# Encoder trunk: the output stages take the two products for the second half of the tokens last, sum them over all blocks in PSUM, and keep their weight forms in DRAM

## The chip, the cores and the metric

One core of one Trainium2 chip. The metric is device time in microseconds for one execution of the whole kernel. The engines are named as in the profile: PE (TensorE), DVE (VectorE), ACT (ScalarE), POOL (GpSimd), SP (SyncE, which issues most DMAs). Three runs of the kernel before gave 2766.35, 2768.74 and 2769.79 us; the median is 2768.74.

## What is computed

Two layers of an encoder on x of shape (1, 1024 tokens, 1024 channels) in float32. The first layer mixes tokens by grouped-query attention (16 heads of 64, 4 key/value heads), the second by a chunked gMLP of width 6144. Each is followed by a dense MLP of hidden width 4096 with a squared ReLU. Every sublayer is preceded by an RMS norm and modulated by vectors that are worked out from the conditioning vector c.

```
for i in range(2):
    mod = silu(c) @ ada_w[i] + ada_b[i]
    sh1, sc1, g1, sh2, sc2, g2 = split(mod, 6)
    h = modulate(rmsnorm(x, norm1_g[i]), sh1, sc1)
    y = gqa_attention(h, ...) if i == 0 else chunked_gmlp(h, ...)
    x = x + g1 * y
    h = modulate(rmsnorm(x, norm2_g[i]), sh2, sc2)
    x = x + g2 * (square(relu(h @ w_in[i])) @ w_out[i])
```

## The kernel before

Every large matmul is done as three products of rounded halves: each float32 operand is split into a rounded part hi (a cast on ACT) and a remainder lo (a subtraction on DVE or POOL), and hi·hi, hi·lo and lo·hi are summed. Around these stands a scheme with seven block products in place of eight (as Strassen and Winograd have it): forms of the operands are added up beforehand, seven products named 1 to 7 are taken, and their sums give the four quarters of the result.

The stages follow each other: QKV, attention, the output projection (`wo`), MLP0's first matmul, MLP0's `Out`, the gMLP's two input products (v, then u), the gMLP's `Out`, MLP1's first matmul, MLP1's `Out`.

**`Out` (L963 to L1110)** is used three times: for MLP0 and MLP1 with 4 blocks of the contraction, for the gMLP with 3. It works in units of 12 matmuls (4 tiles of the contraction times three products; 2.72 us each where TensorE isn't held up, by the starts of successive units in the trace). A unit is named by block b, product q and output pair p of 4. `ahead` issues what is due some units early: `load_w` and `load_w2` fetch the four quarters of a block's weights (11, 12, 21, 22); `prep`, three units ahead (LO), makes the form that the product needs on POOL (L1031 to L1036) and splits it (ACT L1041, DVE L1042); `load_f` and `split_f` fetch a form of the hidden activations from DRAM, eight units ahead, and split it five units ahead (ACT L287, DVE L288). Split activations live in the buffers named t, of which there are 58. `run` issues the matmuls (L1056 hi·hi, L1057 hi·lo, L1058 lo·hi) and `take` (L1082 to L1110) adds a product to the residual x through `add` (L1069, DVE) or to an accumulator in SBUF (L1084, DVE; for the first block an ACT copy). Products 1, 2, 6, 4, 7 serve the first half of the tokens (half 0), and 6 and 7 half 1 as well; 5 and 3 serve half 1 alone. For the blocks ahead of the last two the order is 1264753; the last two take 12647 each, and then 5 and 3 in turns of the two, summed in PSUM. So the last 16 units are the tail: half 0 is complete there, and its next norm begins. `norm_hook` (L1226) does that: at unit HK = 1 of the tail the sums of squares go through TensorE (`norm_ss`, L244, with squares summed on POOL at L235) and DVE (L246 and on), two units later the result is spread over the partitions (`norm_rb`, L255), and then the forms for the next stage are made a step at a time.

**`Slabs` (L159 to L199)** works out four groups of modulation vectors in the attention loop: 4 groups of 8 steps, each a DMA of 512 KB (SP), a multiplication (POOL L184) and an addition (POOL L185, none in a group's first step), and 8 one-column matmuls at a group's end (L194).

**The attention loop (L920 to L956)** runs over 64 units of one head and one pair of query blocks. The order of the work in a unit is written out in the string `ORDER`: near its end stand q (`q_stage`, POOL L811 and L812, in units 1, 5, 9, ...: the split queries that are transposed in the two units from the next one on), f (`f_stage`, POOL L887, a sum of two parts of the output), and m (`slabs.step`). `q_trans` (PE L820) stands early in a unit. Near the end the loop also issues the loads of x (L463) and the first weights of `wo` (L105, cast by ACT at L108).

SP issues DMAs in the order of the program, and waits in it for what a DMA needs. Modulation vectors that are not yet needed stand in `pending` and are made by `mods`, a DMA and two DVE operations of which L145 is the long one, in places written out for each stage (MO: in MLP0's `Out` one in every third unit from the 14th).

Of the kernel before, what the change touches and what calls it, by code (L numbers as in the profile page):

```python
# [11 lines left out]
F32 = mybir.dt.float32  # L12
# [6 lines left out]
P = 128  # L19
# [17 lines left out]
def encoder_kernel(ctx: ExitStack, tc: tile.TileContext, t: dict, out: bass.AP):  # L37
# [121 lines left out]
    class Slabs:  # L159
# [11 lines left out]
        def step(self, bank):  # L171
            self.n += 1
            if self.ends and self.n >= self.ends[0][0]:
                self.end(self.ends.pop(0)[1], bank)
            if not self.work:
                return
            self.ahead(3)
            g, dt = self.work.pop(0)
            raw = self.raw.pop((g, dt))
            if dt == 0:  # L180
                self.acc[g] = wide("s")
                pin(G.tensor_scalar(self.acc[g], raw, condc[:, 0:1], None, ALU.mult))
            else:
                pin(G.tensor_scalar(raw, raw, condc[:, dt : dt + 1], None, ALU.mult))  # L184
                pin(G.tensor_tensor(self.acc[g], self.acc[g], raw, ALU.add))  # L185
            if dt == KT - 1:
                self.ends.append((self.n + 2, g))

        def end(self, g, bank):
            layer, j = g  # L190
# [611 lines left out]
    with ExitStack() as es:  # L802
# [117 lines left out]
        for i in range(nu + 2):  # L920
            u0 = units[i] if i < nu else None
            u1 = units[i - 1] if 0 < i <= nu else None
            u2 = units[i - 2] if i > 1 else None
            if u0:
                if i % 4 == 0:
                    qst, nxt = nxt, []
                u0.qst = qst
            for op in ORDER.split():
                f, w, j = op[0], int(op[1]), int(op[2])
                if f == "m":  # L930
                    if deferred:
                        deferred.pop(0)()
                    elif WO_AT <= i < WO_AT + 10:
                        if i == WO_AT:
                            load_sel()
                        elif i == WO_AT + 1:
                            wo_sums(0)
                        else:
                            wo_prep(0, i - WO_AT - 2)
                    elif i >= nu:  # L940
                        mods(1)
                    if i % 2 or i >= nu:
                        slabs.step(bank_x)
                elif f == "q":
                    if i % 4 == 1 and w == 0 and i + 3 < nu:
                        qh = q_stage(units[i + 3].qq, units[i + 3].g)
                    if i % 4 > 1 and w == 1 and i + 2 < nu:
                        q_trans(qh, i % 4 - 2, nxt)
                else:
                    u = (u0, u1, u2)[w]  # L950
                    if u and (i or f not in "se"):
                        stages[f](u, j)
            if i == nu - 1:
                x[0] = [load_x(0, k) for k in range(KT)]
            if i == nu:
                wo_mm(0, (0,), bank_x)  # L956
# [2 lines left out]

    es_a.close()  # L960
    p_y = ctx.enter_context(tc.tile_pool(name="p_y", bufs=4, space=PSUM))

    class Out:  # L963

# [4 lines left out]
        def __init__(self, wsrc, forms, nblk, gate):  # L969
            self.wsrc, self.forms, self.nblk, self.gate = wsrc, forms, nblk, gate  # L970
            self.n = 28 * nblk
            self.w, self.raw, self.f, self.sf, self.acc = {}, {}, {}, {}, {}
            self.last2 = last2 = (nblk - 2, nblk - 1)
# [16 lines left out]
            tiles = []  # L990
            for i in range(0, self.n - 16, 4):
                tiles += [(i + kt, self.units[i][:2] + (kt,)) for kt in range(4)]
            for i in (self.n - 16, self.n - 8):
                tiles += [(i + 4 * j + kt - FM, (b, self.units[i][1], kt)) for j, b in enumerate(last2) for kt in range(4)]
            for i, k in tiles:
                at(i - FS - FA, self.load_f, k)
            for i, k in tiles:
                at(i - FS, self.split_f, k)
# [28 lines left out]
        def prep(self, i):  # L1027
            b, q, p = self.units[i]
            a11, a12, a21, a22 = (self.w.get((b, c, p)) for c in ("11", "12", "21", "22"))
            if q == "6":  # L1030
                G.tensor_tensor(a21, a21, a22, ALU.add)  # L1031
                G.tensor_tensor(a11, a21, a11, ALU.subtract)
            elif q == "4":
                G.tensor_tensor(a12, a12, a11, ALU.subtract)
            elif q == "7":
                G.tensor_tensor(a22, a22, a11, ALU.subtract)  # L1036
            src = {"1": a11, "2": a12, "6": a11, "4": a22, "7": a22, "5": a21, "3": a12}[q]
# [6 lines left out]
        def run(self, hook=None, done=None):  # L1044
            for i in range(self.n):
                self.ahead(i)
                b, q, p = self.units[i]
                hi, lo = self.sf.pop(i)
                two = q in "53" and b in self.last2
                begin, end = not two or b == self.last2[0], not two or b == self.last2[1]  # L1050
                if begin:
                    ps = (bank_x, bank_y)[(i // 2 if two else i) % 2]("out")
                for kt in range(4):
                    th, tl = self.f[(b, q, kt)]
                    a = slice(kt * P, (kt + 1) * P)
                    T.matmul(ps, hi[:, a], th, start=begin and kt == 0, stop=False)  # L1056
                    T.matmul(ps, hi[:, a], tl, start=False, stop=False)  # L1057
                    T.matmul(ps, lo[:, a], th, start=False, stop=end and kt == 3)  # L1058
                j = i - self.n + 16
# [11 lines left out]
        def take(self, i, b, q, p, ps, done):  # L1071
            acc = self.acc

            def add(hf, j, v):
                self.add(hf, j, p, v)

            if b < self.nblk - 1:
                if q in "243":
                    add(*{"2": (0, 0), "4": (0, 1), "3": (1, 0)}[q], ps)
                elif b == 0:  # L1080
                    acc[(q, p)] = slot()
                    S.copy(acc[(q, p)], ps)  # L1082
                else:
                    V.tensor_tensor(acc[(q, p)], ps, acc[(q, p)], ALU.add)  # L1084
                return
            a1, a6, a5, a7 = (acc[(c, p)] for c in "1657")
            if q == "1":
                V.tensor_tensor(a1, ps, a1, ALU.add)
                add(0, 0, a1)
# [6 lines left out]
                G.tensor_tensor(a7, a7, a6, ALU.add)  # L1096
            elif q == "4":
                add(0, 1, ps)
            elif q == "7":
# [3 lines left out]
            elif q == "5":  # L1103
                V.tensor_tensor(a5, ps, a5, ALU.add)
                add(1, 0, a5)
                add(1, 1, a5)
                done(1, 2 * p + 1)
            else:
                add(1, 0, ps)
                done(1, 2 * p)  # L1110

    OUT_FORMS = "1234567"


    dram = ctx.enter_context(tc.tile_pool(name="dram", bufs=1, space=bass.MemoryType.DRAM))

    def spread(tiles, dst, spare, eng):

# [15 lines left out]
    def mlp(layer, f, sqB, done, hook):  # L1134
# [42 lines left out]
        def at_out(i):  # L1177
# [48 lines left out]
    def norm_hook(layer, which, bank):  # L1226
        dg = []

        def hook(m):
# [161 lines left out]
    def gmlp(f, sqB, done, hook):  # L1391
# [116 lines left out]
        XL = {2: (0, 1), 6: (1, 0), 10: (1, 1)}  # L1508

        def at_out(i):  # L1510
            if i == CUT:
                cut(4)
            if i in XL:
                load_xs(*XL[i])
            if i >= out_.n - 16:
                hook(i - out_.n + 16)

        out_.run(at_out, done)

# [19 lines left out]
FS = 5  # L1539
FA = 3  # L1540
LO = 3
FM = 4
TG = ((0, 0), (1, 0), (1, 1), (0, 1))
MO = (14, 3, 1)
CUT = 8
LW = 5
IG = 30
SW = 3
WA = 6
LW2 = 2  # L1550
HK = 1
HB = 2
HBV = 2
WO_AT = 53
MODS = 32
RO = 1
RQ = 3
RW = 2
NA = (7,)
# [74 lines left out]
```

## Time and profile before

The profiled execution took 2778.2 us (its span in the trace is 2776.4), 9.5 us more than the median of the other three. Its mean TensorE clock was 0.978 of full speed.

| stage | from, us | to, us |
|---|---|---|
| QKV | 0 | 190 |
| attention | 190 | 579 |
| wo | 579 | 693 |
| MLP0 first matmul | 693 | 1015 |
| MLP0 Out | 1015 | 1346.5 |
| gMLP v | 1346.5 | 1596 |
| gMLP u | 1596 | 1877 |
| gMLP Out | 1877 | 2138.8 |
| MLP1 first matmul | 2138.8 | 2460.3 |
| MLP1 Out | 2460.3 | 2776.4 |

A row of a timeline gives the start in us, the duration in us, the engine, the line of the kernel, the operation, its output and inputs with their tiles, the count of like instructions put together, and in brackets the idle time ahead of it and what ended that. A row of waits gives the total, the number of times and the longest. A row of a stretch gives its length, then busy time and count for PE, PEld (weight loads), DVE, ACT and POOL, then the granted clock, the DMA share and GB/s.

### The profile page before, as it was taken

The page shows a single profiled execution, that of the slowest core. Times are in us where ns is not written, and L with a number is a line of the kernel's source. Part 1 is how long each engine was busy: PE and PEld are TensorE (multiplying, and loading weights), DVE is VectorE, ACT ScalarE, POOL GpSimd, SP SyncE. Part 2 cuts the span into 40 slices and gives each one's busy share as a digit, 9 for nine tenths or more (in the row PEclk, how much of TensorE's full clock was granted, in tenths as well). Part 3 has the DMA queues.
Part 4 walks back from the last instruction along what each step waited for, and adds up shares of the span by engine and source line. Part 5 has one row for each costly group of instructions (what it writes and reads, how often), then busy time and mean ns, then how long its engine had stood idle before and what let it go on. Part 6 is the DMA issues. An engine that isn't in the chain of part 4 may idle for free. (4 is left out here: it accounts for less than half of the span.)

```text
span 2776.4 us, 37109 instructions
## 1 busy us (share of the span) xinstructions
PE 2653.8 (96%) x12804; PEld 2195.6 (79%) x12804; DVE 2300.5 (83%) x3231; ACT 1450.6 (52%) x2608; POOL 1054.3 (38%) x716
## 2 busy tenths in 40 slices
PE   7889999999899999998899999999998999999998
PEld 5668999978688888786778888887876688888887
DVE  7889888878887788999997767786899887788896
ACT  4448999954544455434443354444435554554432
POOL 2446666654300023253543255555452400033351
PEclk9999999989999999999999999999998999999999
DMA  7131111235164465734243345555522264465541
GB/s 262 67 137 39 47 47 47 94 113 183 59 211 152 163 235 190 250 112 139 76 137 129 107 164 178 179 196 210 193 84 80 88 208 163 144 247 167 166 136 70
DMA packets 181967, 393.42 MB, mean 142 GB/s; under 512 B 21073, under 2 KB 33361, under 8 KB 181778
## 3 DMA queue, kind: packets, MB, share of 16 engines
q1 hardware_dynamic: 154898, 353.29, 37.6%
q10 hardware_dynamic: 26880, 37.76, 3.7%
q8 instruction: 101, 1.65, 0.2%
q14 instruction: 88, 0.72, 0.1%
HBM read 289.26 MB, written 101.71 MB: 141 GB/s over the span
## 5 line engine op out<-in xcount | busy, mean ns | idle before, releaser
L1057 PE MATMUL out<-t,s 128*128 128x512 f32 x1232 | 487.7, 396 | 14.4 <-DVE t L288 14.2
L1058 PE MATMUL out<-t,s 128*128 128x512 f32 x1232 | 485.6, 394 | 8.3 <-DVE s L1042 8.1
L1056 PE MATMUL out<-t,s 128*128 128x512 f32 x1232 | 484.7, 394 | 3.3 <-ACT t L287 3.3
L415 PE MATMUL w<-t,s 128*128 128x512 f32 x1168 | 460.0, 395 | 0.5 <-ACT t L287 0.5
L416 PE MATMUL w<-t,s 128*128 128x512 f32 x1168 | 455.4, 390 | 1.5 <-DVE t L288 1.3
L417 PE MATMUL w<-t,s 128*128 128x512 f32 x1168 | 454.8, 389 | 0.9 <-DVE s L401 0.9
L288 DVE TENSOR_TENSOR t<-t,t 128x512 fp32r<-128x512 f32 x408 | 383.7, 951 | 42.6 <-ACT t L287 28.9
L287 ACT CAST t<-t 128x512 fp32r<-128x512 f32 x408 | 244.6, 617 | 191.3 <-DVE t L288 80.5
L1031 POOL TENSOR_TENSOR w<-w,t 128x512 f32<-128x512 f32 x32 | 52.8, 1656 | 656.6 <-DMA t<-in_wm_dram 494.3
L1057 PEld LDWEIGHTS out<-t,s 128*128 128x128 f32 x1232 | 234.1, 190 | 70.8 <-DVE t L288 21.6
L1058 PEld LDWEIGHTS out<-t,s 128*128 128x128 f32 x1232 | 234.4, 190 | 61.7 <-DVE s L1042 12.9
L401 DVE TENSOR_TENSOR s<-w,s 128x512 fp32r<-128x512 f32 x292 | 229.5, 794 | 63.2 <-ACT s L400 62.9
L400 ACT CAST s<-w 128x512 fp32r<-128x512 f32 x292 | 172.8, 617 | 200.4 <-PE w L417 123.3
L1056 PEld LDWEIGHTS out<-t,s 128*128 128x128 f32 x1232 | 234.4, 190 | 53.9 <-ACT t L287 5.1
L416 PEld LDWEIGHTS w<-t,s 128*128 128x128 f32 x1168 | 219.4, 188 | 51.4 <-DVE t L288 6.6
L415 PEld LDWEIGHTS w<-t,s 128*128 128x128 f32 x1168 | 219.2, 188 | 49.4 <-issue 3.1
L417 PEld LDWEIGHTS w<-t,s 128*128 128x128 f32 x1168 | 219.2, 188 | 46.3 <-DVE s L401 1.3
L860 DVE TENSOR_TENSOR t<-t,t 128x512 fp32r<-128x512 f32 x256 | 164.0, 681 | 23.5 <-ACT t L854 23.4
L837 DVE TENSOR_REDUCE mx<-s 128x1 f32<-128x1024 f32 x128 | 156.4, 1222 | 27.9 <-PE s L834 26.9
L1042 DVE TENSOR_TENSOR s<-t,s 128x512 fp32r<-128x512 f32 x176 | 163.8, 931 | 15.1 <-ACT s L1041 14.6
L870 PE MATMUL o<-t,t 128*128 128x256 f32 x1024 | 164.9, 294 | 0.0
L851 PE MATMUL t<-ident,c 128*128 128x128 f32 x1024 | 152.4, 278 | 12.7 <-DVE t L860 7.5
(248 smaller groups left out, 5524.9 us busy)
## 6 DMA issues: line engine op xcount, KB each, us to landing
t<-hf SPq DMA_DIRECT2D x320, 256.0 KB, 4.4
hf<-c SPq DMA_DIRECT2D x156, 256.0 KB, 2.1
w<-in_wi_dram SPq DMA_DIRECT2D x64, 512.0 KB, 3.8
hf<-c ACTq DMA_DIRECT2D x96, 256.0 KB, 2.0
c<-in_ada_dram SPq DMA_DIRECT2D x36, 512.0 KB, 3.8
w<-in_adan_dram SPq DMA_DIRECT2D x32, 512.0 KB, 3.3
t<-in_wm_dram SPq DMA_DIRECT2D x64, 256.0 KB, 4.7
w<-in_ada_dram SPq DMA_DIRECT2D x28, 512.0 KB, 4.2
```

What stands on the lines that cost most here:

```text
L287: S.copy(hi, src)
L288: (eng or V).tensor_tensor(lo, src, f32(hi), ALU.subtract)
L400: S.copy(hi, src)
L401: V.tensor_tensor(lo, src, f32(hi), ALU.subtract)
L415: T.matmul(ps, hi[:, a], th, start=kt == 0, stop=False)
L416: T.matmul(ps, hi[:, a], tl, start=False, stop=False)
L417: T.matmul(ps, lo[:, a], th, start=False, stop=kt == 3)
L860: pin(V.tensor_tensor(lo, pt, f32(hi), ALU.subtract))
L870: pin(T.matmul(u.po, vt[st][:, u.g * P : (u.g + 1) * P], src[:, s * 256 : (s + 1) * 256], start=st == 0 and part == 0, stop=st == 7 and pa ...
L1056: T.matmul(ps, hi[:, a], th, start=begin and kt == 0, stop=False)
L1057: T.matmul(ps, hi[:, a], tl, start=False, stop=False)
L1058: T.matmul(ps, lo[:, a], th, start=False, stop=end and kt == 3)
```

## The change

1. **`Out`'s order.** All blocks take 12647 first; then come product 5 over all blocks, the last block first, and product 3 likewise. Each of their four output pairs is summed over the blocks in one PSUM bank that is held through the phase (four of bank_x for 5, four of bank_y for 3). The tail is now 8 units for each block: 32, 24 and 32.
2. **Kept weight forms.** Forms 5 and 3 are made together with 6 and 4, as before, but for all blocks except the last they are stored to DRAM at that time (`keep`) and loaded again 7 units ahead of use (`load_kept`, LK = 4): 24, 16 and 24 stores of 256 KB, and as many loads. Through the sum in PSUM 12 ACT copies and 40 DVE additions are no longer there.
3. **The norm hook.** It begins at unit 3 of the tail (HK) and makes a step of the next stage's forms every second unit to the end.
4. **Slabs.** `step` is called in every unit and works in those with `i * 5 % 8 < 5`, not in the odd ones; a group's end comes three calls later instead of two.
5. **Modulations.** Four of the 16 pending ones move from MLP0's `Out` to the gMLP's (MG).

```
-            if not self.work:
+            if not go or not self.work:
...
-                self.ends.append((self.n + 2, g))
+                self.ends.append((self.n + 3, g))
...
-                    if i % 2 or i >= nu:
-                        slabs.step(bank_x)
+                    slabs.step(bank_x, i * 5 % 8 < 5)
...
-            self.units = [(b, q, p) for b in range(nblk - 2) for q in "1264753" for p in range(4)]
-            self.units += [(b, q, p) for b in last2 for q in "12647" for p in range(4)]
-            self.units += [(b, q, p) for q in "53" for p in range(4) for b in last2]
+            self.units = [(b, q, p) for b in range(nblk) for q in "12647" for p in range(4)]
+            self.units += [(b, q, p) for q in "53" for b in (last, *range(last)) for p in range(4)]
+            self.kept = {(b, q, p): dram.tile([P, 512], F32, name=nm("wf"))
+                         for b in range(last) for q in "53" for p in range(4)}
...
+                elif q in "53" and b < last:
+                    at(i - LO - LK, self.load_kept, b, q, p)
...
+        def load_kept(self, *k):
+            self.w[k] = slot()
+            nc.sync.dma_start(self.w[k], self.kept[k])
+
+        def keep(self, b, q, p, a):
+            if b < self.nblk - 1:
+                nc.sync.dma_start(self.kept[(b, q, p)], a)
+            else:
+                self.w[(b, q, p)] = a
...
             if q == "6":
                 G.tensor_tensor(a21, a21, a22, ALU.add)
+                self.keep(b, "5", p, self.w.pop((b, "21", p)))
                 G.tensor_tensor(a11, a21, a11, ALU.subtract)
             elif q == "4":
                 G.tensor_tensor(a12, a12, a11, ALU.subtract)
+                self.keep(b, "3", p, self.w.pop((b, "12", p)))
...
-                two = q in "53" and b in self.last2
-                begin, end = not two or b == self.last2[0], not two or b == self.last2[1]
+                last = self.nblk - 1
+                begin, end = q not in "53" or b == last, q not in "53" or b == last - 1
                 if begin:
-                    ps = (bank_x, bank_y)[(i // 2 if two else i) % 2]("out")
+                    self.ps[(q, p)] = (bank_x, bank_y)[{"5": 0, "3": 1}.get(q, i % 2)]("out")
...
-            if pending and i >= MO[0] and (i - MO[0]) % MO[1] < MO[2]:
+            if len(pending) > 4 and i >= MO[0] and (i - MO[0]) % MO[1] < MO[2]:
...
-            if hook and i >= out_.n - 16:
-                hook(i - out_.n + 16)
+            if hook and i >= out_.n - out_.tail:
+                hook(i - out_.n + out_.tail)
...
-                more(fg[-1], (m % 2) if m < 12 else RO, None)
+                more(fg[-1], m % 2, None)
...
+MG = (16, 4, 1)
-HK = 1
+HK = 3
+LK = 4
```

The program's order on POOL in the attention loop, units 6 to 9 (a row is the line, the operation, output and inputs, and the shape; L887 is `f_stage`, L184 and L185 are a slab, L811 and L812 the `q_stage` of unit 9). Before:

```order
L887 TENSOR_TENSOR t_2221<-t_2223,t_2221 64x256
L887 TENSOR_TENSOR t_2221<-t_2305,t_2221 64x256
L184 TENSOR_SCALAR w_1971<-w_1971,condc 128x1024
L185 TENSOR_TENSOR s_1790<-s_1790,w_1971 128x1024
L887 TENSOR_TENSOR t_2383<-t_2385,t_2383 64x256
L811 CAST t_2462<-t_1115 128x4x64
L811 CAST t_2465<-t_1122 128x4x64
```

The same place after the change:

```order
L887 TENSOR_TENSOR t_2225<-t_2227,t_2225 64x256
L887 TENSOR_TENSOR t_2225<-t_2309,t_2225 64x256
L184 TENSOR_SCALAR w_2058<-w_2058,condc 128x1024
L185 TENSOR_TENSOR s_1723<-s_1723,w_2058 128x1024
L887 TENSOR_TENSOR t_2387<-t_2389,t_2387 64x256
L184 TENSOR_SCALAR w_2143<-w_2143,condc 128x1024
L185 TENSOR_TENSOR s_1723<-s_1723,w_2143 128x1024
L811 CAST t_2470<-t_1115 128x4x64
L811 CAST t_2473<-t_1122 128x4x64
```

A second slab (w_2143) now stands between the last `f_stage` and `q_stage`; the transposes on PE keep their place.

DVE around the norm hook of MLP0's `Out` (L1069, after the change L1089, adds to x; L1042, after it L1058, is the lo part of a weight form; L288 the lo part of an activation form; L246 is DVE's first step behind the sums of squares). Before:

```order
L1069 SCALAR_TENSOR_TENSOR x_7181<-t_11177,mod,x_7181 128x512
L1042 TENSOR_TENSOR s_13272<-c_12605,s_13272 128x512
L1069 SCALAR_TENSOR_TENSOR x_7185<-t_11201,mod,x_7185 128x512
L288 TENSOR_TENSOR t_13197<-t_13113,t_13196 128x512
L288 TENSOR_TENSOR t_13220<-t_13140,t_13219 128x512
L1104 TENSOR_TENSOR t_11227<-out_13203,t_11227 128x512
L246 TENSOR_SCALAR ms_13249<-ss_13244 128x4
```

After the change:

```order
L1089 SCALAR_TENSOR_TENSOR x_7181<-t_11231,mod,x_7181 128x512
L288 TENSOR_TENSOR t_12812<-t_12721,t_12811 128x512
L1058 TENSOR_TENSOR s_12894<-t_12778,s_12894 128x512
L1089 SCALAR_TENSOR_TENSOR x_7185<-t_11257,mod,x_7185 128x512
L288 TENSOR_TENSOR t_12841<-t_12751,t_12840 128x512
L1058 TENSOR_TENSOR s_12919<-t_12807,s_12919 128x512
L288 TENSOR_TENSOR t_12866<-t_12780,t_12865 128x512
L288 TENSOR_TENSOR t_12891<-t_12809,t_12890 128x512
L1058 TENSOR_TENSOR s_12966<-t_12836,s_12966 128x512
L288 TENSOR_TENSOR t_12916<-t_12838,t_12915 128x512
L246 TENSOR_SCALAR ms_12941<-ss_12936 128x4
```

Between the last addition to x and L246 there are six splits of forms now, where there were two and an addition.

PE in MLP0's tail after the change, where product 3 goes over from the last block to the first (units 100 and 101 of 112; L1073, L1074, L1075 are hi·hi, hi·lo, lo·hi; out_13302 and out_13326 are two output pairs, the tiles t the split form, 13350 its fourth):

```order
L1075 MATMUL out_13302<-t_13319,s_13323 128x512
L1073 MATMUL out_13326<-t_13260,s_13354 128x512
...
L1075 MATMUL out_13326<-t_13295,s_13354 128x512
L1073 MATMUL out_13302<-t_13350,s_13323 128x512
L1073 MATMUL out_13326<-t_13319,s_13354 128x512
L1074 MATMUL out_13326<-t_13320,s_13354 128x512
L1074 MATMUL out_13302<-t_13351,s_13323 128x512
```

Where the tail of before began (product 7 of block 3, then product 5 of block 2; L1056 to L1058 are the same three products):

```order
L1056 MATMUL out_13176<-t_13035,s_13092 128x512
L1057 MATMUL out_13176<-t_13036,s_13092 128x512
L1058 MATMUL out_13176<-t_13035,s_13092 128x512
L1056 MATMUL out_13203<-t_12954,s_13119 128x512
L1057 MATMUL out_13203<-t_12955,s_13119 128x512
L1058 MATMUL out_13203<-t_12954,s_13119 128x512
```

Before, a unit's twelve matmuls stand together; after, the next unit's are put between those of unit 100, whose fourth form (13350, 13351) is split last.

More of the change, by code (lines that the diff above doesn't have):

```diff
@@ L169, in ahead, with step @@
                 nc.sync.dma_start(self.raw[(g, dt)], t["adan"][g[0], g[1], dt])
-        def step(self, bank):
+        def step(self, bank, go):
             self.n += 1
@@ L961, in encoder_kernel @@
     p_y = ctx.enter_context(tc.tile_pool(name="p_y", bufs=4, space=PSUM))
+    dram = ctx.enter_context(tc.tile_pool(name="dram", bufs=1, space=bass.MemoryType.DRAM))
     class Out:
@@ L971, in __init__ @@
             self.n = 28 * nblk
-            self.w, self.raw, self.f, self.sf, self.acc = {}, {}, {}, {}, {}
-            self.last2 = last2 = (nblk - 2, nblk - 1)
-            self.units = [(b, q, p) for b in range(nblk - 2) for q in "1264753" for p in range(4)]
-            self.units += [(b, q, p) for b in last2 for q in "12647" for p in range(4)]
-            self.units += [(b, q, p) for q in "53" for p in range(4) for b in last2]
+            self.tail = 8 * nblk
+            self.w, self.raw, self.f, self.sf, self.acc, self.ps = {}, {}, {}, {}, {}, {}
+            last = nblk - 1
+            self.units = [(b, q, p) for b in range(nblk) for q in "12647" for p in range(4)]
+            self.units += [(b, q, p) for q in "53" for b in (last, *range(last)) for p in range(4)]
+            self.kept = {(b, q, p): dram.tile([P, 512], F32, name=nm("wf"))
+                         for b in range(last) for q in "53" for p in range(4)}
             todo = []
@@ L989, in __init__ @@
                         at(i - LO - (LW if b else LW2), self.load_w2, b, "21", p // 2)
[L990 to L998, printed above, removed]
+                elif q in "53" and b < last:
+                    at(i - LO - LK, self.load_kept, b, q, p)
+            for i in range(0, self.n, 4):
+                for kt in range(4):
+                    at(i + kt - FS - FA, self.load_f, self.units[i][:2] + (kt,))
+            for i in range(0, self.n, 4):
+                for kt in range(4):
+                    at(i + kt - FS, self.split_f, self.units[i][:2] + (kt,))
             for i in range(self.n):
@@ L1034, in prep @@
                 G.tensor_tensor(a12, a12, a11, ALU.subtract)
+                self.keep(b, "3", p, self.w.pop((b, "12", p)))
             elif q == "7":
                 G.tensor_tensor(a22, a22, a11, ALU.subtract)
-            src = {"1": a11, "2": a12, "6": a11, "4": a22, "7": a22, "5": a21, "3": a12}[q]
+                del self.w[(b, "11", p)], self.w[(b, "22", p)]
+            src = self.w.pop((b, q, p)) if q in "53" else {"1": a11, "2": a12, "6": a11, "4": a22, "7": a22}[q]
             w_ = wide("s", F32R)
@@ L1048, in run @@
                 hi, lo = self.sf.pop(i)
-                two = q in "53" and b in self.last2
-                begin, end = not two or b == self.last2[0], not two or b == self.last2[1]
+                last = self.nblk - 1
+                begin, end = q not in "53" or b == last, q not in "53" or b == last - 1
                 if begin:
-                    ps = (bank_x, bank_y)[(i // 2 if two else i) % 2]("out")
+                    self.ps[(q, p)] = (bank_x, bank_y)[{"5": 0, "3": 1}.get(q, i % 2)]("out")
+                ps = self.ps[(q, p)] if not end else self.ps.pop((q, p))
                 for kt in range(4):
@@ L1058, in run @@
                     T.matmul(ps, lo[:, a], th, start=False, stop=end and kt == 3)
-                j = i - self.n + 16
+                if p == 3:
+                    for kt in range(4):
+                        del self.f[(b, q, kt)]
+                j = i - self.n + self.tail
                 if 0 <= j < 8:
@@ L1075, in add @@
                 self.add(hf, j, p, v)
+            if q == "5":
+                add(1, 0, ps)
+                add(1, 1, ps)
+                done(1, 2 * p + 1)
+                return
+            if q == "3":
+                add(1, 0, ps)
+                done(1, 2 * p)
+                return
             if b < self.nblk - 1:
-                if q in "243":
-                    add(*{"2": (0, 0), "4": (0, 1), "3": (1, 0)}[q], ps)
+                if q in "24":
+                    add(*{"2": (0, 0), "4": (0, 1)}[q], ps)
                 elif b == 0:
@@ L1085, in take @@
                 return
-            a1, a6, a5, a7 = (acc[(c, p)] for c in "1657")
+            a1, a6, a7 = (acc[(c, p)] for c in "167")
             if q == "1":
@@ L1098, in take @@
                 add(0, 1, ps)
-            elif q == "7":
+            else:
                 V.tensor_tensor(a7, ps, a7, ALU.add)
@@ L1102, in take @@
                 done(0, 2 * p + 1)
[L1103 to L1110, printed above, removed]
     OUT_FORMS = "1234567"
-    dram = ctx.enter_context(tc.tile_pool(name="dram", bufs=1, space=bass.MemoryType.DRAM))
     def spread(tiles, dst, spare, eng):
@@ L1510, in at_out @@
         def at_out(i):
-            if i == CUT:
+            if i == MG[0] - 6:
                 cut(4)
+                load_cond(cwide())
+            elif pending and i == MG[0] - 2:
+                silu_cond()
+            if pending and i >= MG[0] and (i - MG[0]) % MG[1] < MG[2]:
+                mods(1, "c")
             if i in XL:
                 load_xs(*XL[i])
-            if i >= out_.n - 16:
-                hook(i - out_.n + 16)
+            if i >= out_.n - out_.tail:
+                hook(i - out_.n + out_.tail)
         out_.run(at_out, done)
@@ L1541 @@
 LO = 3
-FM = 4
 TG = ((0, 0), (1, 0), (1, 1), (0, 1))
 MO = (14, 3, 1)
-CUT = 8
+MG = (16, 4, 1)
 LW = 5
@@ L1555 @@
 MODS = 32
-RO = 1
 RQ = 3
```

## The prediction

> **What bounds the kernel now.** I read the page's busy table and clock slices first, then the busy times by stage, and only then single places.
>
> ```profile
> span 2776.4 us, 37109 instructions
> PE 2653.8 (96%) x12804; PEld 2195.6 (79%) x12804; DVE 2300.5 (83%) x3231; ACT 1450.6 (52%) x2608; POOL 1054.3 (38%) x716
> ...
> PEclk9999999989999999999999999999998999999999
> ```
>
> TensorE is busy 96% of the span, so the change can win only from the remaining 4% and from stretches at a lower clock; what it adds to TensorE's idle time it pays in full. Its matmul count hardly changes. So I ask, stage by stage, where TensorE idles. The stages that the diff touches, in the view by stretches (length; busy time and instructions of PE, PEld, DVE, ACT, POOL; granted clock; DMA share; GB/s), are the attention loop and the three `Out` stages:
>
> ```profile
> 250.00:561.00 311.00, 310.90 (x2295) 287.43 (x2294) 269.19 (x335) 284.49 (x567) 205.03 (x161) 1.00 0.17 56
> 1015.30:1346.50 331.20, 315.77 (x1356) 256.80 (x1356) 306.47 (x412) 154.67 (x272) 133.30 (x85) 0.98 0.53 182
> 1877.00:2138.80 261.80, 244.19 (x1021) 196.25 (x1020) 221.99 (x273) 118.76 (x210) 114.41 (x76) 0.95 0.43 148
> 2460.30:2776.40 316.10, 306.46 (x1345) 251.58 (x1343) 261.85 (x333) 132.58 (x236) 115.87 (x72) 1.00 0.44 149
> ```
>
> In attention TensorE is busy for 310.9 of 311.0 us at full clock: nothing can be won there, and a wait put in there lengthens the span by itself. The three `Out` stages leave 15.4, 17.6 and 9.6 us idle, beside some half clock: that is all the change can win.
>
> **Part 1, the slabs in attention (cost).** The change is written for `Out`, but one edit is in the attention loop: `Slabs.step` runs in 5 of 8 units (`i * 5 % 8 < 5`) and no longer in the odd ones. POOL works in the order of the program. `q_stage` (L811, L812) stands in units 1, 5, 9, ... and TensorE's transposes of it (L820) early in the next unit. All multiples of 4 satisfy the new rule, so a slab now stands in the unit right before every `q_stage`, until the 32 slabs are used up at about unit 50. Before, that unit was even and had none. In the trace of before, POOL (start, duration, line):
>
> ```profile
> 252.11 2.85 POOL L184 TENSOR_SCALAR w<-w,condc 128x1024 f32<-128x1024 f32 x1
> ...
> 257.38 0.75 POOL L887 TENSOR_TENSOR t<-t,t 64x256 f32<-64x256 f32 x1
> 258.07 0.75 POOL L811 CAST t<-t 128x256 fp32r<-128x256 f32 x2
> 258.77 1.44 POOL L812 TENSOR_TENSOR t<-t,t 128x256 fp32r<-128x256 f32 x2
> ```
> ```profile
> 262.20 0.53 PE L820 MATMUL qt<-identr,t 128*128 128x128 f32 x4
> ```
>
> A slab holds POOL from 252.11 to 257.38: 5.27 us. `q_stage` ends at 258.77 + 1.44 = 260.21, 1.99 us before TensorE takes it up at 262.20. That is all the slack there is. Two cases follow.
> (a) Where the two units before `q_stage` both have a slab (transposes in units 10, 18, 26, 34, 50), the second one is added to this chain: 5.27 - 1.99 = 3.3 us of wait, five times.
> (b) Where only the last has one (14, 22, 30, 38, 42, 46), the attention output's sum (L887) no longer waits behind a slab but starts when its data come:
>
> ```profile
> 273.94 0.72 POOL L887 TENSOR_TENSOR t<-t,t 64x256 f32<-64x256 f32 x1 [4.80 <-ACT t L882]
> 274.77 2.85 POOL L184 TENSOR_SCALAR w<-w,condc 128x1024 f32<-128x1024 f32 x1
> ...
> 280.04 0.74 POOL L887 TENSOR_TENSOR t<-t,t 64x256 f32<-64x256 f32 x1
> ...
> 284.94 0.73 POOL L887 TENSOR_TENSOR t<-t,t 64x256 f32<-64x256 f32 x1 [2.09 <-ACT t L882]
> ```
> ```profile
> 284.85 0.54 PE L820 MATMUL qt<-identr,t 128*128 128x128 f32 x4
> ```
>
> The first and last of these were released by their data, two units apart, so the middle one's data came at about 279.4. From there: 0.8 for the sum, 5.27 slab, 2.14 `q_stage`: 287.6 instead of 284.85, 2.8 us late, six times. Together 5 x 3.3 + 6 x 2.8 = **+33 us**. Behind the waiting transposes stand all matmuls of the unit, and TensorE has no idle time in which to catch up. Units 2 and 6 I cost at nothing: there the slab only changes places with the rotary work.
>
> **Part 2, the clock after these waits (cost).** The same stage, a little earlier, shows what a wait of that size does:
>
> ```profile
> 234.78 0.92 PE L851 MATMUL t<-ident,c 128*128 128x128 f32 x4 [2.42 <-DVE t L860]
> ```
> ```profile
> 231.50:235.00 3.50, 1.08 (x10) 0.88 (x9) 3.50 (x4) 0.78 (x1) 3.42 (x4) 1.00 0.32 102
> 235.00:238.50 3.50, 3.50 (x16) 3.22 (x15) 2.64 (x4) 3.22 (x8) 3.09 (x6) 0.51 0.12 48
> ```
>
> After an idle time of 2.42 us TensorE ran 3.5 us at 0.51 of its clock and lost 1.7 us by it. Eleven times that is **+19 us**. The ends: nothing (MLP1's `Out` has waits up to 2.2 us, in the list further down, and a clock of 1.00), and 5.2 us each, or 57, by the longest half-clock stretch below. I take 1.7, since the nearest row is of this stage and its wait the nearest in size. The Trainium skill ("TensorE: Matmul & The Clock Gate", section "HAM oscillation — how this bites in real kernels") says that "The abstract rule is 'no PE-idle gaps >~3.4µs.'" By that rule all my waits are too short to lower the clock, and this term would be zero; the rows just shown, half clock after 2.42 us, disagree with it.
>
> **Part 3, the end of attention (small gain).**
>
> ```profile
> 549.47 1.75 SPq L463 DMA_DIRECT2D x<-in_xT_dram  x4
> 561.56 0.33 SPq L105 DMA_DIRECT2D w<-in_wo_dram  x1
> ```
> ```profile
> 564.90 1.04 ACT L108 CAST s<-w 128x1024 fp32r<-128x1024 f32 x1 [4.22 <-DMA w<-in_wo_dram]
> ```
> ```profile
> 567.21 1.11 PE L851 MATMUL t<-ident,c 128*128 128x128 f32 x4 [3.93 <-DVE t L860]
> ```
> ```profile
> 566.10:576.40 10.30, 9.19 (x33) 7.86 (x34) 6.22 (x8) 7.88 (x15) 7.10 (x4) 0.50 0.15 51
> ```
>
> A late load of `wo` holds ACT for 4.22 us, that starves TensorE for 3.93, and 10.3 us at half clock follow: some 9 us lost. With the slabs done at unit 50, SP reaches these loads earlier, but then they queue right behind the loads of x. I take **-3 us** of a possible -9 to 0.
>
> **Part 4, the `Out` tails (gain).** The hook's sums of squares (L244) come two units of 2.72 us after the last "7" unit before, four after. The squares are POOL's (L235):
>
> ```profile
> 1302.38 1.87 PE L244 MATMUL ss<-ones,t 128*128 128x1 f32 x8 [6.21 <-POOL t L235]
> ```
> ```profile
> 2095.58 1.65 PE L244 MATMUL ss<-ones,t 128*128 128x1 f32 x7 [6.39 <-POOL t L235]
> ```
> ```profile
> 1300.00:1310.20 10.20, 7.82 (x22) 6.50 (x23) 7.48 (x15) 4.80 (x9) 1.58 (x1) 0.50 0.52 178
> 2091.90:2102.10 10.20, 6.52 (x19) 5.51 (x20) 9.43 (x17) 4.82 (x8) 2.27 (x2) 0.50 0.06 12
> ```
>
> Two units more, 5.44 us, leave 0.8 and 0.95 of the waits 6.21 and 6.39: **-11 us**. The half clock behind them goes too. Less the wait inside each stretch (10.2 - 7.82 and 10.2 - 6.52), half of what remains is 3.9 and 3.3: **-7 us**. What is late next is the hook's second product (L255), which waits for DVE work that now has DVE's form splits ahead of it: **+4 us**, 2 for each hook, between nothing and the 3.8 that it waited elsewhere (below).
>
> The waits on DVE in the three `Out` stages (total, times, longest; the first three are of MLP0's, gMLP's and MLP1's), and the costs of what leaves DVE and what joins the DMA queues:
>
> ```profile
> PE out L1057 <- DVE t L288: 6.1, 5, 1.9
> PE rb L255 <- DVE t L250: 3.8, 1, 3.8
> ```
> ```profile
> PE out L1057 <- DVE t L288: 7.5, 6, 2.4
> PE w L415 <- ACT t L287: 4.1, 2, 2.6
> ```
> ```profile
> PE out L1058 <- DVE s L1042: 5.0, 4, 2.2
> ```
> ```profile
> L1084 DVE TENSOR_TENSOR t<-out,t 128x512 f32<-128x512 f32 x68 | 46.2, 679 | 2.2 <-PE out L1058 2.2
> ```
> ```profile
> t<-hf SPq DMA_DIRECT2D x320, 256.0 KB, 4.4
> ```
>
> DVE loses 40 operations of about 0.68 us, 27 of its 790 us in these stages. That is work beside TensorE; what counts is the waits, 18.6 us in these three rows. A third of them: **-6 us** (0 to -18.6). Against it, the program's order shows seven places in the new tails, where a block's forms begin, at which a form is split right when TensorE needs it (before: three or more units earlier), because all buffers named t are taken. At the mean wait of such a row, 6.1 / 5 = 1.2 us, that is **+8 us** (0 to 7 x 2.4 = 17). The next stages start with fewer conversions queued on DVE: **-5 us** of the rows for L255 and L415 (0 to -7.9).
>
> At nothing: the 64 stores and 64 loads of kept forms. One of 256 KB lands in 4.4 us (the last row), and a load is issued seven units, 19 us, before its use; the DMA share of these stages is 0.53 at most. The stores wait for POOL, and SP's queue behind them with them. If POOL ran more than 15 us late there, each load would show; nothing suggests it at 133 busy of 331 us. The twelve ACT copies that go and the four modulations that move are hidden too: ACT is half idle, and DVE's share of gMLP's stage is 0.85.
>
> **The sum.** 33 + 19 - 3 - 11 - 7 + 4 - 6 + 8 - 5 = **+32 us** on a span of 2776.4. The profiled execution took 2778.2, and the median of the runs shown is 2768.74, 9.5 below it; I add the sum to the median: **2801 us**. About 0.2%, 2763.2 to 2774.3, can't be told from no change.
>
> **The rivals.**
> R1, the waits come without the half clock: +13, **2782 us**. For it speaks MLP1's `Out` and the skill's rule; against it the two rows of part 2. Chance 0.14.
> R2, the other side: the waits in attention don't arise, because another slab than the one in front of `q_stage` is hidden in POOL's idle time (POOL is busy 205 of 311 us). The price is then parts 3 and 4 alone, -20: **2749 us**. It decides at one point: that `q_stage` ends no more than 1.99 us later than now. Against it: POOL's idle time lies behind `q_stage`, not ahead of it, and nothing in the order lets it pass the slab. Chance 0.13.
> R3, the worse side: half clock twice as long after each wait (+19 more), and the late splits at their upper end (+9 more): **2829 us**. Chance 0.11. That the kept forms come late, so that the change doesn't do what it says, would look the same in the tails.
> R4, cancelling: half of the waits, no half clock: 32 - 19 - 16 = -3, **2766 us**. Chance 0.05.
>
> **How the numbers follow.** The forecast has 0.57. The range 2764 to 2834 holds it, R1, R4 and most of R3; R2 is left out. Faster by over 0.2%: R2 and a little of R4, 0.14. Within: R4 and the low side of R1, 0.08. Slower: 0.78.
>
> **What would show it.** Right: transposes L820 waiting for POOL's L812 eleven times, 33 us in total; every fourth unit up to the 50th 2.8 us or more longer; clock dips in the attention slices; the 6 us waits of L244 on L235 gone; in the tails the first product of a block's unit waiting for L288. Wrong: a TensorE still 99% busy in attention (R2); waits without dips (R1); loads of kept forms as releasers (R3).

## The result, and the profile after

The changed kernel takes 2792.55 us (median of four runs, 2788.94 to 2797.24) against 2769.26 for the kernel before (four runs, 2766.35 to 2769.95). The ratio is 1.0087, with a 95% interval from 1.0070 to 1.0105: 23 us slower. The forecast was 2801.

The head of the page of the changed kernel, with the clock slices:

```profile
span 2790.5 us, 37339 instructions
PE 2661.6 (95%) x12804; PEld 2195.3 (79%) x12804; DVE 2269.1 (81%) x3191; ACT 1459.8 (52%) x2598; POOL 1061.5 (38%) x716
...
PEclk9899999999999999999999999999999999999999
```

TensorE's instructions are the same in number, DVE has its 40 fewer and is busy 31 us less, and the span is longer: the change took work away from an engine that did not set the end. What TensorE waited for, over the whole span (total, times, longest), is a new first row and a few smaller shifts. First the rows of the kernel before:

```profile
PE out L1057 <- DVE t L288: 14.2, 12, 2.4
PE ss L244 <- POOL t L235: 12.6, 2, 6.4
...
PE rb L255 <- DVE t L250: 8.2, 2, 4.4
PE out L1058 <- DVE s L1042: 8.1, 7, 2.2
...
PE t L851 <- DVE t L860: 7.5, 4, 3.9
...
PE out L1056 <- ACT t L287: 3.3, 4, 1.1
```

And the same view of the changed kernel:

```profile
PE qt L820 <- POOL t L812: 30.2, 24, 5.4
PE out L1074 <- DVE t L288: 14.5, 15, 2.0
PE out L1073 <- ACT t L287: 8.8, 9, 1.6
PE rb L255 <- DVE t L250: 8.5, 2, 4.4
...
PE out L1075 <- DVE s L1058: 5.9, 8, 2.1
...
PE t L851 <- DVE t L860: 1.1, 3, 0.6
```

The wait of the transposes for `q_stage`, which the kernel before has not among its rows, is 30.2 us. The waits of the sums of squares (L244) for POOL are gone, the waits of `Out`'s matmuls for splits and weight forms have grown a little (25.6 us in three rows before, 29.2 after), and those of L851 on L860, of which 3.9 us stood at the end of attention, are nearly gone.

The table gives each stage from its first matmul to the first of the next, in us, from the traces of the two kernels and of three of the experiments below:

| stage | before | after | e3 | e8 | e13 |
|---|---|---|---|---|---|
| QKV | 185.8 | 185.1 | 184.4 | 186.0 | 186.0 |
| attention and wo | 503.0 | 539.0 | 495.4 | 496.2 | 494.2 |
| MLP0 first matmul | 326.3 | 323.8 | 326.6 | 324.0 | 324.2 |
| MLP0 Out | 331.0 | 329.7 | 328.7 | 326.5 | 319.6 |
| gMLP v | 250.0 | 243.2 | 242.5 | 250.5 | 246.4 |
| gMLP u | 281.0 | 281.1 | 281.1 | 281.1 | 281.1 |
| gMLP Out | 261.6 | 254.8 | 252.7 | 254.9 | 249.6 |
| MLP1 first matmul | 321.6 | 316.5 | 316.3 | 320.9 | 316.3 |
| MLP1 Out | 316.1 | 317.2 | 316.8 | 317.1 | 313.8 |

Attention costs 36 us more; everything else together gains 22. The profiled executions differ by 14 us and the medians by 23, because the profiled execution of before was itself 9 us above its median. Which stage held those 9 us can't be told from one trace, so the experiments are judged by their timed runs, as ratios to the kernel before on the same chip (its median there was 2773.7 for e1 to e4, 2772.4 for e5, e7, e8 and e10, 2773.2 for e11 to e13, 2771.7 for e14).

This is the place in attention that the prediction worked out, POOL in the changed kernel:

```profile
254.06 0.73 POOL L887 TENSOR_TENSOR t<-t,t 64x256 f32<-64x256 f32 x1 [5.16 <-ACT t L882]
254.89 2.85 POOL L184 TENSOR_SCALAR w<-w,condc 128x1024 f32<-128x1024 f32 x1
257.82 2.38 POOL L185 TENSOR_TENSOR s<-s,w 128x1024 f32<-128x1024 f32 x1
260.17 0.73 POOL L887 TENSOR_TENSOR t<-t,t 64x256 f32<-64x256 f32 x1
260.89 2.84 POOL L184 TENSOR_SCALAR w<-w,condc 128x1024 f32<-128x1024 f32 x1
263.81 2.37 POOL L185 TENSOR_TENSOR s<-s,w 128x1024 f32<-128x1024 f32 x1
266.12 0.74 POOL L811 CAST t<-t 128x256 fp32r<-128x256 f32 x2
266.82 1.41 POOL L812 TENSOR_TENSOR t<-t,t 128x256 fp32r<-128x256 f32 x2
```

and PE beside it:

```profile
264.60 0.60 PE L851 MATMUL t<-ident,c 128*128 128x128 f32 x4
267.60 0.28 PE L820 MATMUL qt<-identr,t 128*128 128x128 f32 x1 [2.40 <-POOL t L812]
268.29 0.62 PE L820 MATMUL qt<-identr,t 128*128 128x128 f32 x3 [0.40 <-POOL t L812]
```

Two slabs stand one behind the other, and `q_stage` ends at 266.82 + 1.41 = 268.23. TensorE was done with its other work at 265.2. It waits twice, since the first transpose needs only the first of the two tiles that L812 makes. The stretches around it (columns as before), and those around a wait of 1.73 us at 323.0 that had another end:

```profile
264.00:268.30 4.30, 1.49 (x12) 1.07 (x10) 2.02 (x3) 1.46 (x5) 4.23 (x5) 1.00 0.26 87
268.30:271.70 3.40, 3.40 (x14) 2.91 (x15) 0.17 (x1) 2.28 (x4) 0.73 (x1) 0.50 0.11 45
319.20:323.10 3.90, 2.17 (x15) 1.76 (x13) 2.86 (x4) 2.30 (x5) 3.90 (x5) 1.00 0.14 23
323.10:326.50 3.40, 2.99 (x23) 2.64 (x24) 0.98 (x1) 2.31 (x5) 1.24 (x2) 1.00 0.33 128
```

After the first, 3.4 us at half clock (a granted clock of 0.50); after the second, none.

### The profile page after: what moved, and what is told of

It reads as the page before. It is cut to its first block, busy times and chain, and to the rows that moved or that the text cites. A ratio compares the mean times of both kernels' runs of the same rounds, so it can differ in the third digit from the quotient of the medians.

```text
span 2790.5 us, 37339 instructions
## 1 busy us (share of the span) xinstructions
PE 2661.6 (95%) x12804; PEld 2195.3 (79%) x12804; DVE 2269.1 (81%) x3191; ACT 1459.8 (52%) x2598; POOL 1061.5 (38%) x716
## 5 line engine op out<-in xcount | busy, mean ns | idle before, releaser
L1074 PE MATMUL out<-t,s 128*128 128x512 f32 x1232 | 486.8, 396 | 14.5 <-DVE t L288 14.5
L1073 PE MATMUL out<-t,s 128*128 128x512 f32 x1232 | 487.8, 396 | 8.8 <-ACT t L287 8.8
L1075 PE MATMUL out<-t,s 128*128 128x512 f32 x1232 | 485.9, 395 | 6.1 <-DVE s L1058 5.9
L288 DVE TENSOR_TENSOR t<-t,t 128x512 fp32r<-128x512 f32 x408 | 376.8, 937 | 29.4 <-ACT t L287 21.9
L287 ACT CAST t<-t 128x512 fp32r<-128x512 f32 x408 | 244.6, 618 | 154.5 <-DMA t<-hf 63.3
L1074 PEld LDWEIGHTS out<-t,s 128*128 128x128 f32 x1232 | 234.8, 191 | 70.9 <-DVE t L288 21.8
L1073 PEld LDWEIGHTS out<-t,s 128*128 128x128 f32 x1232 | 234.7, 191 | 62.9 <-ACT t L287 13.9
L1075 PEld LDWEIGHTS out<-t,s 128*128 128x128 f32 x1232 | 234.7, 191 | 59.8 <-DVE s L1058 11.1
L1058 DVE TENSOR_TENSOR s<-t,s 128x512 fp32r<-128x512 f32 x240 | 216.0, 901 | 51.8 <-ACT s L1057 51.5
L1057 ACT CAST s<-t 128x512 fp32r<-128x512 f32 x240 | 147.9, 621 | 190.9 <-PE out L1075 115.4
L860 DVE TENSOR_TENSOR t<-t,t 128x512 fp32r<-128x512 f32 x256 | 164.9, 684 | 22.2 <-ACT t L854 21.8
L854 ACT CAST t<-t 128x512 fp32r<-128x512 f32 x256 | 145.3, 592 | 39.5 <-PE t L851 37.1
```

Of the source, the lines that this page charges most:

```text
L287: S.copy(hi, src)
L288: (eng or V).tensor_tensor(lo, src, f32(hi), ALU.subtract)
L860: pin(V.tensor_tensor(lo, pt, f32(hi), ALU.subtract))
L1058: V.tensor_tensor(lo, src, f32(hi), ALU.subtract)
```

## The experiments

Theory A, the prediction's: the slab ahead of `q_stage` costs more than all the rest gains, and the rest gains some 13 to 22 us. Rivals: much of the loss sits in the tails or in the added DMA (B), or POOL can't do five slabs in eight units wherever they stand (C).

**e1 and e2: the change without its slabs, and its slabs without the rest.** e1 is the changed kernel with

```
-                    slabs.step(bank_x, i * 5 % 8 < 5)
+                    if i % 2 or i >= nu:
+                        slabs.step(bank_x, True)
...
-                self.ends.append((self.n + 3, g))
+                self.ends.append((self.n + 2, g))
```

and e2 the kernel before with the change's lines at these places.

> The changed kernel with the slabs of before (odd units, a group's end two calls later); everything else of the change stays. Theory A (the slab ahead of q_stage is the whole loss, the Out stages and what follows them gain 13 to 22 us): 2747 to 2756 us, no waits of L820 on L812. Rival B (a good part of the loss lies elsewhere, in the tails or the added DMA): 2770 to 2790.

> The kernel before with the slabs of the change alone (5 of 8 units, end three calls later). Theory A: 30 us of waits of L820 on L812 and some ten half-clock stretches in attention, 2800 to 2810 us. Rival B: less than half of it, 2775 to 2785.

e1 took 2754.91 us, ratio 0.9931 (0.9918 to 0.9944): 19 us faster than before. e2 took 2813.4, ratio 1.0143 (1.0127 to 1.0158): 40 us slower, above the expected 2800 to 2810 as it stands and within it by the ratio (40 us on 2769 are 2809). Its first row of waits:

```profile
PE qt L820 <- POOL t L812: 28.4, 23, 3.9
```

The two halves add up: -19 + 40 = +21, beside +23 measured for the whole. B is out: without the new slabs the change is a gain.

**e3, e4 and e10: as many slabs, at other places.** e3 is the changed kernel, e4 the kernel before (with a group's end three calls later, as in the change), both with slabs in units that are not right ahead of `q_stage`:

```
-                    slabs.step(bank_x, i * 5 % 8 < 5)
+                    slabs.step(bank_x, i % 8 in (1, 2, 3, 5, 6))
```

e10 leaves the change's slabs and takes `q_stage` a unit earlier:

```
-                    if i % 4 == 1 and w == 0 and i + 3 < nu:
-                        qh = q_stage(units[i + 3].qq, units[i + 3].g)
+                    if i % 4 == 0 and w == 0 and i + 4 < nu:
+                        qh = q_stage(units[i + 4].qq, units[i + 4].g)
```

> The changed kernel with slabs in units 1, 2, 3, 5 and 6 of every 8: as many slabs in as many units, none in the unit right ahead of q_stage. Theory A (the place of the slab decides): no waits of L820 on L812, and the late loads at the end of attention stay gone, so some 8 us better than with the old slabs: 2739 to 2748 us. Rival C (POOL can't do 5 slabs in 8 units without holding up attention, wherever they stand): 2780 to 2795, waits of L820 or of L851 stay.

> The kernel before with slabs in units 1, 2, 3, 5 and 6 of every 8 and nothing else of the change. Theory A: only the end of attention changes, 9 us better at most: 2760 to 2766 us, against 2769 before. Rival C: 2790 to 2810.

> The changed kernel with its own slabs, but q_stage one unit earlier (units 0, 4, 8, ...), so that a slab no longer stands between it and the transposes that need it. Theory A (only the order on POOL decides): no waits of L820 on L812, 2739 to 2750 us. Rival C (five slabs in eight units are too many for POOL): 2775 or more.

e3 took 2745.49 us, ratio 0.9903 (0.9889 to 0.9918); e4 2765.68, ratio 0.9976 (0.9964 to 0.9987); e10 2745.43, ratio 0.9889 (0.9869 to 0.9910). In e10 no transpose waits for POOL; in e3, where none was expected, two still do:

```profile
PE qt L820 <- POOL t L812: 2.1, 2, 1.7
```

C is out: POOL has time for five slabs in eight units, as long as none stands between `q_stage` and its deadline. e4 also gives the price of the late loads at the end of attention, which the earlier end of the slabs removes: 7 us by the ratio (4 to 10 by its interval), 8 by the medians.

**e5: the norm hook at unit 1 again.** The edit is `HK = 1` in e3.

> The changed kernel with slabs off q_stage (as e3_slabs_off_q, 2745 us beside 2774 before) and the norm hook again at unit 1 of the tail, two units after the last product 7. Theory of the prediction's part 4 (the two units more removed 11 us of waits and half clock behind them): L244 waits for POOL's L235 again, 5 to 6 us at two places, each with half clock behind it, 2756 to 2763 us. Rival (the longer tail has other work between, or another wait takes its place): within 3 us of 2745.

It took 2747.33 us, ratio 0.9902 (0.9886 to 0.9918): no different from e3. The wait that was to come back, outside attention:

```profile
PE ss L244 <- POOL t L235: 0.9, 1, 0.9
```

The theory falls: in the changed kernel the two 6 us waits do not go because the hook stands two units later. In the traces L244 starts 12.0 and 12.6 us after the last product 7 in the kernel before, two units and the wait, and 12.3 and 12.0 us after it in e5, where it waits only once, 0.9 us. There the two units ahead of it take that long by themselves: in MLP0's tail TensorE is held up in them by late splits (waits of 1.72 and 1.37 us for L288, and half clock), and the squares are ready by then. So the time seems to have moved from one wait to the other. That is a reading of the traces; an early hook without late splits was not tried.

**e8: the next stage's forms late.** In e3 the hook's steps behind its norm are put into the last 16 units of the tail:

```
-                hook(i - out_.n + out_.tail)
+                j = i - out_.n + out_.tail
+                if j <= HK + 2 or j - out_.tail + 16 > HK + 2:
+                    hook(j if j <= HK + 2 else j - out_.tail + 16)
...
-                more(fg[-1], m % 2, None)
+                more(fg[-1], m % 2 if m < 10 else 1, None)
```

> As e3_slabs_off_q, with the hook's steps for the next stage's forms in the last 16 units of the tail, as before the change, not from its start on. Theory (the forms hold buffers t and so make the splits late): the waits on L287 and L288 from the fifth block of the tail on go, those at its start stay, 0 to 4 us faster, 2741 to 2745. Rival (the splits are late for another reason): the same waits, 2745, or slower where the next stage starts later.

It took 2755.96 us, ratio 0.9935 (0.9920 to 0.9951), 9 us slower than e3 by the ratios. The waits that were to go stayed: `Out`'s matmuls waited 15.1 us for L288 and 6.4 for L287, where in e3 they waited 16.5 and 5.6. So this theory falls too: the forms are not what makes the splits late. MLP0's `Out` gained 2 us in its trace, but the gMLP's v stage and MLP1's first matmul went back to 250.5 and 320.9 us, near the 250.0 and 321.6 of the kernel before (table). At the start of v in e8:

```profile
PE rb L255 <- DVE t L250: 5.8, 1, 5.8
PE ss L244 <- DVE t L235: 2.3, 1, 2.3
```

In e3 the second of these rows isn't there and the first is 4.1. So the 12 us that the change gains in these two stages come from forms that are ready earlier, which the long tail gives room for.

**e7, e11 and e12: the added DMA.** e7 does each store and each load of a kept form twice. e11 leaves the stores out, and its loads take a raw quarter of the weights, so it computes something else. e12 stores twice, the second time to another tensor:

```
 def keep(self, b, q, p, a):
     if b < self.nblk - 1:
         nc.sync.dma_start(self.kept[(b, q, p)], a)
+        nc.sync.dma_start(self.kept2[(b, q, p)], a)
```

> As e3_slabs_off_q, with each store and each load of a kept weight form done twice (64 stores and 64 loads of 256 KB more). Theory (the DMA of the change is hidden): within 3 us of 2745. Rival (it delays the loads of activation forms and so the splits): 2750 to 2765, more waits of the matmuls on L287 and L288.

> As e3_slabs_off_q (ratio to before 0.9903), but without the 64 stores of kept forms; the loads stay, and take a raw quarter of the weights instead of the stored form (so products 5 and 3 of all blocks but the last use other numbers than the reference). Theory D (the added DMA costs in proportion, so that e7's +16 us for doubling says what the change itself pays): 5 to 10 us faster than e3, ratio 0.987 or less. Theory E (e7 paid for its own order: its second store and load wait on SP for the first, and hold up what is queued behind): ratio 0.990, within 3 us of e3.

> As e3_slabs_off_q, with each kept form stored twice, the second time to another place in DRAM, so that no store waits for another; loads as they are. Theory D: 5 to 8 us slower than e3, ratio 0.9925 or more. Theory E: within 3 us of e3, ratio 0.990.

e7 took 2761.55 us, ratio 0.9953 (0.9938 to 0.9968): 14 us slower than e3 by the ratios, against the theory that the DMA is hidden; `Out`'s matmuls waited 22.1 us for L288 and 10.4 for L287, where in e3 they waited 16.5 and 5.6. But its trace shows a wait that is the experiment's own. The queue of SP, from 940 to 2300 us (L1025 is the second load, L1030 the second store):

```profile
SPq L1025 <- DMA t<-wf: 51.7, 32, 4.2
SPq L1030 <- DMA wf<-w: 45.3, 30, 4.1
```

Each second transfer to the same place waits on SP for the first, and every later load is held up behind it. e12, which doubles the stores without that wait, took 2747.56 us, ratio 0.9910 (0.9894 to 0.9927): within 2 us of e3. So 16 MB more of stores cost nothing that shows. e7's loss is then most likely that of a queue that stands still; e12 has no second loads, so their bytes are not excluded. e11 took 2740.78 us, ratio 0.9879 (0.9862 to 0.9896). That is 7 us under e3 by the ratios and 5 by the medians, but the two intervals still touch (e3 from 0.9889). The stores as they stand may cost a few microseconds, then not by their bytes; the wait of SP's queue for POOL's form ahead of each store is the candidate (in e3's trace 57.1 and 33.0 us in the two main rows), and was not taken apart.

**e13 and e14: the splits earlier.** The edit is one number, in e3 (e13) and in the kernel before (e14):

```
-FS = 5
+FS = 8
```

> As e3_slabs_off_q, with the activation forms split 8 units ahead instead of 5 (loaded 11 ahead). If the buffers t are what makes the splits of the tails late, as the prediction had it, nothing changes: ratio 0.990, the same waits on L287 and L288. If it is only the lead (the conversions queue on DVE behind other work of the tail), the waits in the tails go, and their half clock: 6 to 12 us faster than e3, ratio 0.986 to 0.988.

> The kernel before with the activation forms split 8 units ahead instead of 5 and nothing else. If the late splits belong to the change's longer tails, this gains little: ratio to before 0.997 to 1.001. If the kernel before had them as well (its five waits on L288 in MLP0's Out, six in the gMLP's, with half clock behind some), it gains as e13 did over e3: ratio 0.994 to 0.996.

e13 took 2732.99 us, ratio 0.9853 (0.9835 to 0.9870), e14 2758.88, ratio 0.9956 (0.9942 to 0.9969). In e13 `Out` has no waits for L287 or L288 any more (22.1 us in e3). What is left in it is the weight forms, above all their lo part, and these waits have grown from 7.5 us in e3 to 19.1: part of the time has only moved (waits from 900 to 2760 us):

```profile
PE out L1075 <- DVE s L1058: 19.1, 22, 1.8
PE rb L255 <- DVE t L250: 4.8, 1, 4.8
...
PE ss L244 <- POOL t L235: 2.6, 2, 1.5
```

So the buffers t are not what made the splits late: there is room for three more units of lead. The last row bears on e5. Without the late splits the four units ahead of the hook take their 10.9 us, and L244 waits for its squares again:

```profile
1244.33 0.49 PE L244 MATMUL ss<-ones,t 128*128 128x1 f32 x3 [1.48 <-POOL t L235]
```

And the kernel before had the same trouble: it gains 12 us, where e13 gains 12 to 14 over e3. There the waits of the sums of squares, 12.6 us before, grow instead:

```profile
PE ss L244 <- POOL t L235: 16.2, 2, 9.2
```

e13 beats both kernels: 1.5% under the kernel before, by the change with its slabs elsewhere and with the longer lead.

## Why the prediction was right

It was right in the sign and in what decides it. Its +32 us are 9 more than the 23 measured, and these lie in attention: slabs, clock and the end of attention were put at 33 + 19 - 3 = 49 us, and e2 measures the three together as 40. The rest was put at -17 and measured as -19, but there luck had a part.

**The slabs (+33 us).** Right in its mechanism and its places: the waits come in units 10, 14, 18 and so on to 50, and e1, e2, e3 and e10 show that it is the slab in front of `q_stage` and not the number of slabs. The sum of the waits is 30.2 us, with 0.3 of it at the end of QKV and 5.7 (5.41 and 0.32) in unit 6, which the prediction had costed at nothing ("the slab only changes places with the rotary work"); there it stands behind the rotary work and delays `q_stage` as well. The eleven others come to about 24 instead of 33. Unit 10 is late by 268.2 - 265.2 = 3.0 us where 3.3 were worked out, part of which the rows don't count as waits, since the first transpose starts when its own tile is there. Unit 42 waited only 0.4 us, because the one-column matmuls of a group's end (L194) had taken TensorE 1.84 us shortly before and so put its transposes off.

**The clock (+19 us).** Right in kind: of the eleven waits eight are followed by 3.4 us at half clock, 1.7 us each, and unit 6's goes with 6.8 us, 2.6 of them within the wait itself. That is 8 x 1.7 = 14 us in place of 19, and some 2 in unit 6. Units 18 and 46 had their waits without it, and their length shows the price: 8.4 us each, where units 14 and 22 with half clock took 10.0.

**The end of attention (-3 us).** Mis-sized: -7 to -8 us by e4. The loads do queue behind those of x, but the wait on L860 at this place fell from 3.93 us to under 0.7 all the same, and the 10.3 us at half clock went. So did another 6.8 us at half clock that followed at 600.3 us, in `wo`, which the prediction had not listed.

**The tails.** The terms of part 4 came to -17 us and e1 measured -19, but several of them were wrong and made up for each other. That the sums are so near is luck.
- The waits of L244 (-11): they went, even all 12.6 us of them, but the step "Two units more, 5.44 us" was not the reason. e5 put the hook back and they stayed away. The arithmetic holds where nothing else stops TensorE: in e13 the two waits are 1.5 and 1.2 us, where the prediction left 0.8 and 0.95. What it missed, as the traces read, is that this term and the late splits are not separate: a split that holds up the units ahead of the hook uses up the time in which the hook would have waited.
- The half clock behind them (-7): the step failed. Those stretches went and others came at the late splits of the tail's first units. Over the three `Out` stages half clock came to 39 us before, 38 after and 27 in e3, whose `Out` is the same: a gain of 1 us in one trace and 6 in the other. The stretches after the change:

```profile
1285.40:1292.20 6.80, 5.67 (x13) 4.10 (x14) 6.80 (x10) 3.21 (x6) 2.82 (x3) 0.50 0.65 224
2087.60:2094.40 6.80, 6.03 (x14) 4.36 (x15) 6.80 (x9) 3.35 (x7) 2.83 (x3) 0.50 0.35 117
```

DVE is busy through both, TensorE isn't. Having put a price on the late splits' waits, the prediction had none on the clock behind them, though its own part 2 has half clock after a wait of 2.42 us.
- The next product of the hook (+4): L255 waited 8.5 us instead of 8.2, so nothing.
- DVE's relief and the late splits (-6 + 8): the waits on splits and weight forms rose from 25.6 to 29.2 us, +3.6 for +2. But the cause given, "because all buffers named t are taken", is wrong, as e13 shows, and the kernel before had the same kind of waits, as e14 shows.
- The next stages (-5): mis-sized, -12 us (250.0 to 243.2 and 321.6 to 316.5). e8 shows why: the long tail brings the forms forward, a gain for which the prediction had only part of the existing waits as its measure.
- The DMA at nothing: the stores' bytes cost nothing that can be told (e12); the loads' bytes were not tried alone, and whether the stores' waits on SP cost a few microseconds stays open (e11).

The stage lengths leave 5 us of attention's 36 unassigned: 30.2 of waits, 6.8 of half clock more than before (44.2 us of it against 30.6, halved), 6.4 less of L860's waits make 31. Of the rivals, R2 asked for the one thing that decides, a `q_stage` no more than 1.99 us later. Counted from the L887 ahead of the first slab (251.29 us before, 254.06 after, the release of both being ACT's L882), it ended 8.9 us on before and 14.2 after, so 5.3 us later.

## What to carry to other kernels

When the cadence of a filler is changed on an engine that works in order, look for the instruction with the least slack that it may land in front of; here 2 us of slack, measured in one place of the trace, decided the sign of the whole change. An edit that comes along with a large one, a constant or a modulus, deserves its own line in the sum: the main part of this change was worth 19 us, and a line that looked like housekeeping cost 40. And where an engine that feeds the critical one runs close to full, try the lead of its work before the amount: three units more of lead gave some 12 us to both kernels, while with 40 operations fewer on that engine the waits of `Out`'s matmuls for it went only from 22.3 to 20.4 us.

## What the runs showed of the hardware

The clock of TensorE falls after shorter waits than the 2.42 us that the prediction went by, and not always. Waits of 1.74 us at L820, with 0.41 us more behind the next transpose, were followed by 3.4 us at half clock at 294.4, 348.2, 404.3 and 458.3 us, and by none at 323.0 and 510.4. The Trainium skill ("TensorE: Matmul & The Clock Gate", section "What's actually happening") says that the window over which the activity is judged runs free of the kernel. The trace agrees: the same wait falls on either side. Over the whole span half clock came to 123 us in the kernel before, 118 in the changed one, 80 in e3 and 64 in e13. Half of the difference between the first and e3 is 22 us, two thirds of the 32 us by which e3's profiled span is shorter than that of before.
